# Places for slots, PSUM banks and temporaries by a minimum-cost matching, and a search from kept states, in a hybrid decoder trunk

## The chip, the cores and the metric

The kernel runs on one core of one Trainium2 chip. The metric is device microseconds of one execution. For the kernel before it is the median of three runs. A profile is of one further execution.

A core has five engines that work side by side, each with its own queue of instructions in a fixed order: TensorE (PE, matrix products, with weight loads shown apart as PEld), VectorE (DVE), ScalarE (ACT), GpSimd (POOL) and SyncE (SP, which issues the DMAs here). They wait for each other through semaphores. Matrix products land in PSUM, which has eight banks of 128x512 float32; all else lies in SBUF.

## The reference

Two layers (L = 2) on x of 1024 positions and 1024 channels, all in float32:

```python
for l in range(DEPTH):
    h = rmsnorm(x, attn_norm[l])
    proj = h @ w_in[l]          # 1952 columns, split among four mixers
    y_a = mla_attention(...)    # 4 heads, latent queries and keys, rotary part, causal
    y_b = short_gated_conv(...) # width 3
    y_c = multiscale_pool(...)  # windows 2, 4, 8, 16
    y_d = swa_sink_attention(...)  # window 128, ALiBi, sinks
    mixed = rmsnorm of each of the four groups, times mix_norm[l]
    x = x + mixed @ w_o[l]
    h2 = rmsnorm(x, ffn_norm[l])
    gate, up = jnp.split(h2 @ w_gate_up[l], 2, axis=-1)   # 2 x 2816 columns
    x = x + (jax.nn.silu(gate) * up) @ w_down[l]
return rmsnorm(x, final_norm)
```

## The kernel before

**Data.** Channels lie on the 128 partitions, positions in the free dimension, in two halves (t = 0 and 1) of 512. Every float32 operand of a product is split into a high part, rounded to the format `float32r` of PE, and a low part, the rest. `split` (L299 to L310) makes the high part on ACT (L301, or L306 with a gain) and the low part on DVE (L304, or L307); weights of the attention stage are split in `weights` (ACT L223, DVE L224). One product is then three matmuls, high x high, high x low and low x high: `mm3`, whose matmul is L281. Its sums lie in PSUM under the names `ps_mm`, `ps_s`, `ps_t` and `ps_pv`.

**Stages.** A layer is an attention stage and a feed-forward stage. In the first, PE computes input projections, sliding-window attention (L594 to L655), latent attention (scores L999 to L1001, transposes L1053, values L1065) and the output projection, with many softmax, rotation and split steps on DVE and ACT between them: L380 (products), L1004 and L1007 (maxima), L1018 and L1021 (exponentials), L1037 (scaling). The feed-forward products are made as seven products of 2x2 blocks (B11, B21, B22, N1, N2, T3, T4), whose sums of operands are made ahead: `combine` and `combine_rest` (L1169 to L1186) for the activations, POOL for the weights (L1247, L1249, L1277, L1539). The Silu is at L1459. The end is a last square sum (L364, L368), the last norm (L370 to L376) and the scaling by it (L428).

**Storage.** Three kinds of tiles are given places while the program is written down:

- 47 *slots* of 128x1024 float32 (`u0` to `u46`, shown as `u` in the profile), taken as pairs or halves from the class `Slots` (L57);
- eight PSUM *banks*, by `ps` (L182);
- eight *temporaries* of 128x512, by `tmp` (L191), in three rings: two named `te`, three `tn`, three `tp`. A ring gives its tiles in turn.

A tile that takes a place must wait until the last reader of the tile that had the place is done. So the choice of places decides which waits there are beside those for data.

**The order.** The program is written down once in the order of the code; then a planner makes the order of every engine's queue. The class `Order` (L2103) takes each instruction's duration from formulas (`costs`, L2209, in us), for example these for DVE:

```python
elif op in ("TensorTensor", "TensorReduce"):
    t = 0.15 + n * 0.001045
```

where n is the number of elements of a row. ACT's casts from SBUF are 0.18 + n * 0.00085, a change of ACT's function table is 1.28. `_forward` (L1851) then runs the whole program in a model of five engines. It is used in two ways: with ranks, when each engine takes the ready instruction of the lowest rank, or with fixed orders. `find` (L2255) passes forward and backward to get first ranks; `banks` (L2281) and `spans` (L2296) then give banks and slots from the planned times; the program is written down again with them, and `_search` (L2015) tries changes of the ranks: every second trial lowers the ranks of a chain of instructions that ends at a gap of PE, the other ones shake the ranks in a stretch anywhere in the span. A trial is kept when the mean of the planned ends, over four draws of random delays of the DMAs, is lower. Five rounds of this with 150 trials each are made, and the best of them is searched with 1500 (`TRIALS`, L1808; 40 without the compiler `numba`). The order found is laid upon the queues (`impose`).

A place is chosen greedily before: of the places that are free by the planned start of a tile, the one that came free last; where none is, the one that comes free first (L76 for slots, L291 for banks).

Of the kernel before, what the change touches and what calls it, by code (L numbers as in the profile page):

```python
# [6 lines left out]

# [49 lines left out]
class Slots:  # L57

    def __init__(self, pool, n, spans=None):
        self.pool = pool
        self.spans = spans
        self.made = []
        self.until = [0.0] * n
# [3 lines left out]
        self.dt = [None] * n  # L69

    def place(self):

        if self.spans is None:
            return self.places.popleft()
        start, end = self.spans[len(self.made)]
        i = max(self.places, key=lambda i: u if (u := self.until[i]) <= start else -u)  # L76
        self.places.remove(i)
        self.until[i] = end
        return i

    def pair(self, dt):
        i = self.place()
        self.cur[i] = self.pool.tile([P, 2, HT], dt, name=f"u{i}", tag=f"u{i}", bufs=1)
        self.made.append(self.cur[i].name)
        self.dt[i] = dt
        return 2 * i
# [9 lines left out]
    def free(self, i):  # L96
        h = self.halves[self.dt[i // 2]]
        if i ^ 1 in h:
            h.remove(i ^ 1)
            self.places.append(i // 2)  # L100
        else:
            h.append(i)

    def free_pair(self, i):
        self.places.append(i // 2)
# [25 lines left out]
def trunk_kernel(ctx: ExitStack, tc: tile.TileContext, ins, out, given=None, spans=None, made=None):  # L131
# [10 lines left out]
    slots = Slots(ctx.enter_context(tc.tile_pool(name="slots", bufs=1)), N_U, spans)  # L142
    if made is not None:
        made.append(slots.made)
# [1663 lines left out]
TRIALS = 1500 if numba else 40  # L1808
# [42 lines left out]
def _forward(eng, kind, seen, taken, kb, want, late, hop, start, to, sync, count, rank, fixed, order):  # L1851

    n = eng.size
    left = count.copy()
    ready = np.zeros(n)
    end = np.zeros(n)
    begin = np.zeros(n)
    free = np.zeros(5)
    lk, lv = np.zeros((5, n)), np.zeros((5, n), np.int64)
    nk, nv = np.zeros((5, n)), np.zeros((5, n), np.int64)  # L1860
    ln, nn = np.zeros(5, np.int64), np.zeros(5, np.int64)
    done = np.zeros(5, np.int64)
    flying = np.zeros(LANES)
    issued = 0
    served = 0.0
    lock = 0.0
    table = 0
    for k in range(n):
        if left[k] == 0:
            e = eng[k]  # L1870
            _push(lk[e], lv[e], ln[e], 0.0, k)
            ln[e] += 1
    for _ in range(n):
        best, b = 1e18, -1
        for e in range(5):
            if fixed:
                if done[e] == 0:
                    pass
                i = done[e]
                k = order[e, i] if i < order.shape[1] else -1  # L1880
                if k < 0 or left[k] > 0:
                    continue
                t = max(free[e], ready[k])
            else:
                while ln[e] > 0 and lk[e, 0] <= free[e]:
                    k = lv[e, 0]
                    _drop(lk[e], lv[e], ln[e])
                    ln[e] -= 1
                    _push(nk[e], nv[e], nn[e], rank[k], k)
                    nn[e] += 1  # L1890
                if nn[e] > 0:
                    t = free[e]
                elif ln[e] > 0:
                    t = lk[e, 0]
                else:
                    continue
            if e == SP and issued >= LANES:
                t = max(t, flying[issued % LANES])
            if t < best:
                best, b = t, e  # L1900
        if b < 0:
            return end, begin, False
        t, e = best, b
        if fixed:
            k = order[e, done[e]]
        else:
            while ln[e] > 0 and lk[e, 0] <= t:
                k = lv[e, 0]
                _drop(lk[e], lv[e], ln[e])
                ln[e] -= 1  # L1910
                _push(nk[e], nv[e], nn[e], rank[k], k)
                nn[e] += 1
            k = nv[e, 0]
            _drop(nk[e], nv[e], nn[e])
            nn[e] -= 1
            order[e, done[e]] = k
        done[e] += 1
        more = 0.0
        if kind[k] >= TWO:
            get = max(t + 0.08, lock)  # L1920
            more = get - t - 0.08
            lock = get + max(0.05, seen[k] - (0.16 if kind[k] == TWO else 0.19))
        elif e == ACT and want[k] >= 0:
            if want[k] != table:
                more = 0.0 if kind[k] == TABLE else 1.29
                table = want[k]
        begin[k] = t
        free[e] = t + taken[k] + more
        end[k] = t + seen[k] + more
        if e == SP:  # L1930
            served = max(t + (1.31 if kind[k] == LOAD else 0.41), served) + kb[k] / 322.0
            end[k] = served + 0.82 + late[k]
            flying[issued % LANES] = end[k]
            issued += 1
        for i in range(start[k], start[k + 1]):
# [5 lines left out]
            if left[j] == 0 and not fixed:  # L1941
                _push(lk[eng[j]], lv[eng[j]], ln[eng[j]], ready[j], j)
                ln[eng[j]] += 1
    return end, begin, True
# [51 lines left out]
def _trials(arrays, graph, lates, order, limit):  # L1996

    eng, kind, seen, taken, kb, want, hop = arrays
    start, to, sync, count = graph[:4]
    none = np.zeros(0)  # L2000
    total = 0.0
    for s in range(lates.shape[0]):
        end, _, ok = _forward(
            eng, kind, seen, taken, kb, want, lates[s], hop, start, to, sync, count, none, True, order
        )
        if not ok:
            return 1e18
        total += end.max()
        if total + (lates.shape[0] - 1 - s) * (limit - 2.0) > lates.shape[0] * limit:
            return 1e18  # L2010
    return total / lates.shape[0]
# [3 lines left out]
def _search(arrays, graph, lates, margin, rank, trials, seed):  # L2015
# [5 lines left out]
    width = 0  # L2021
    for e in range(5):
        width = max(width, (eng == e).sum())
    order = -np.ones((5, width), np.int64)
    end, begin, _ = _forward(
        eng, kind, seen, taken, kb, want, margin, hop, start, to, sync, count, rank, False, order
    )
    best = _trials(arrays, graph, lates, order, 1e9)
    first = best
    wins = 0  # L2030
    rank = begin
    trial = -np.ones((5, width), np.int64)
    before = -np.ones(n, np.int64)
    for it in range(trials):
        new = rank.copy()
        if it % 2:
            lo = np.random.random() * end.max()
            hi = lo + math.exp(np.random.random() * 3.5 + 0.7)
            s = math.exp(np.random.random() * 4.0 - 1.5)
            some = np.random.randint(0, 10)  # L2040
            for k in range(n):
                if lo <= begin[k] < hi and (some >= 5 or eng[k] == some):
                    new[k] += s * np.random.randn()
        else:
            last = -1
            gaps = 0.0
            for q in range(width):
                k = order[PE, q]
                if k < 0:
                    break  # L2050
                if last >= 0:
                    gap = begin[k] - begin[last] - taken[last]
                    if gap > 0.04:
                        gaps += gap
                last = k
            pick = np.random.random() * gaps
            last, k = -1, -1
            for q in range(width):
                k = order[PE, q]
                if last >= 0:  # L2060
                    gap = begin[k] - begin[last] - taken[last]
                    if gap > 0.04:
                        pick -= gap
                        if pick <= 0:
                            break
                last = k
            for e in range(5):
                last = -1
                for q in range(width):
                    j = order[e, q]  # L2070
                    if j < 0:
                        break
                    before[j] = last
                    last = j
            s = math.exp(np.random.random() * 4.5 - 1.5)
            for _ in range(np.random.randint(3, 40)):
                new[k] -= s
                p, t = before[k], -1.0
                if p >= 0:
                    t = begin[p] + taken[p]  # L2080
                for i in range(bstart[k], bstart[k + 1]):
                    j = bto[i]
                    r = end[j] + hop[eng[k]] if bsync[i] else begin[j]
                    if r > t:
                        p, t = j, r
# [3 lines left out]
        e1, b1, _ = _forward(  # L2089
            eng, kind, seen, taken, kb, want, margin, hop, start, to, sync, count, new, False, trial  # L2090
        )
        if e1.max() > end.max() + 1.5:
# [390 lines left out]
```

## Time and profile before

| | |
|---|---|
| median of 3 runs | 2044.93 us (2044.12 to 2046.39) |
| the profiled execution's own time | 2045.38 us |
| its span, first to last instruction | 2043.6 us |
| mean granted clock of PE | 0.997 |
| busy: PE, DVE, ACT, POOL | 2022.9, 1578.5, 998.8, 438.9 us |
| instructions (all records) | 26485 |
| DMA traffic | 308.13 MB, mean 151 GB/s |

A line of a group or a wait names the engine, the tile it writes and the line of the code. The line is that of the helper, so L281 stands for nearly all matmuls and L301 and L304 for nearly all splits. "Idle before" is the time for which an engine stood before an instruction, and behind the arrow is what ended it. A row of the timeline begins with the time since the start of the span and the duration. The granted clock is 1 at full speed.

### The profile page before, as it was taken

To read this page: it belongs to the slowest core of one execution; us is meant where nothing else is said; L and a number is where in the kernel's file an instruction comes from. 1 tells how busy PE (TensorE), PEld (TensorE's weight loads), DVE (VectorE), ACT (ScalarE), POOL (GpSimd) and SP (SyncE) were. 2 spreads that over 40 slices of the span, in tenths; PEclk is the share of its full clock that TensorE was granted. 3 is DMA by queue.
4 is the path that set the end of the run, shared out by engine and by line. 5 is a ranking of instruction groups with operands and counts; after the bars stand their busy time and mean duration, and the time that the engine had idled before them with its cause. 6 is when DMAs were issued, how large, how long until landed. Compare 5 with 4: busy or idle time off the path is not lost. (4 is left out here: it accounts for less than half of the span.)

```text
span 2043.6 us, 26485 instructions
## 1 busy us (share of the span) xinstructions
PE 2022.9 (99%) x9398; PEld 1672.6 (82%) x9398; DVE 1578.5 (77%) x2553; ACT 998.8 (49%) x1753; POOL 438.9 (21%) x340
## 2 busy tenths in 40 slices
PE   9999999999999999999999999999999999999998
PEld 7888788878888888888888878888788888888887
DVE  8989979998677777655657999799977777776555
ACT  7458657743333334444434576577433333354342
POOL 0300000025565661000003000000356556500000
PEclk9999999999999999999999999999999999999999
DMA  6310223435555556766513112243455555487542
GB/s 244 127 44 21 84 63 110 149 128 179 179 177 183 176 188 246 259 211 222 176 38 128 56 27 78 65 134 119 145 191 186 177 173 191 169 296 235 195 161 98
DMA packets 144133, 308.13 MB, mean 151 GB/s; under 512 B 14080, under 2 KB 61184, under 8 KB 144000
## 3 DMA queue, kind: packets, MB, share of 16 engines
q1 hardware_dynamic: 144000, 306.43, 44.4%
q8 instruction: 74, 1.21, 0.2%
q14 instruction: 59, 0.48, 0.1%
HBM read 215.67 MB, written 89.65 MB: 149 GB/s over the span
## 5 line engine op out<-in xcount | busy, mean ns | idle before, releaser
L281 PE MATMUL ps_mm<-u,u 128*128 128x512 f32 (+1 forms) x3374 | 843.5, 390 | 7.0 <-ACT u L301 2.8
L281 PEld LDWEIGHTS ps_mm<-u,u 128*128 128x128 f32 x3374 | 615.4, 189 | 129.7 <-ACT u L301 3.6
L281 PE MATMUL ps_s<-u,u 128*128 128x512 f32 x2724 | 652.0, 389 | 0.2 <-DVE u L1214 0.2
L281 PEld LDWEIGHTS ps_s<-u,u 128*128 128x128 f32 x2724 | 510.9, 188 | 108.1 <-DVE u L1214 0.6
L301 ACT CAST u<-u 128x1024 fp32r<-128x1024 f32 (+2 forms) x426 | 361.8, 868 | 478.0 <-PE ps_s L281 116.3
L304 DVE TENSOR_TENSOR u<-u,u 128x1024 fp32r<-128x1024 f32 (+2 forms) x426 | 461.3, 1100 | 154.7 <-ACT u L301 107.0
L281 PE MATMUL ps_t<-u,u 128*128 128x512 f32 (+1 forms) x1092 | 251.9, 377 | 0.0
L281 PEld LDWEIGHTS ps_t<-u,u 128*128 128x128 f32 x1092 | 196.1, 188 | 39.1 <-DVE te L380 0.5
L281 PE MATMUL ps_pv<-u,u 128*128 128x512 f32 x696 | 167.4, 389 | 0.0
L281 PEld LDWEIGHTS ps_pv<-u,u 128*128 128x128 f32 x696 | 130.6, 188 | 27.3 <-DVE tp L1670 0.3
L1277 POOL TENSOR_TENSOR u<-u 128x512 f32<-128x512 f32 x38 | 73.3, 1928 | 226.9 <-DVE u L304 174.2
L1459 ACT ACTIVATE tp<-tp 128x512 f32<-128x512 f32 x76 | 48.0, 632 | 129.3 <-DVE tp L380 129.3
L1062 POOL MEMSET u<- 128x128 f32 x32 | 6.0, 214 | 471.9 <-PE ps_mm L281 250.9
L1247 POOL TENSOR_TENSOR u<-u,u 128x512 f32<-128x512 f32 x38 | 55.6, 1464 | 205.5 <-PE ps_s L281 109.2
L770 POOL TENSOR_TENSOR u<-u,u 128x512 f32<-128x512 f32 x6 | 8.0, 1337 | 413.1 <-ACT sm L628 326.4
L301 ACT CAST u<-ps_t 128x512 fp32r<-128x512 f32 (+3 forms) x132 | 64.8, 502 | 41.3 <-PE ps_t L643 16.6
L1539 POOL TENSOR_TENSOR u<-u 128x352 f32<-128x352 f32 x64 | 79.5, 1244 | 22.4 <-DMA u<-in_w_dn 18.7
L304 DVE TENSOR_TENSOR u<-ps_t,u 128x512 fp32r<-128x512 f32 (+3 forms) x132 | 75.2, 580 | 11.4 <-ACT u L301 10.7
L306 ACT ACTIVATE u<-u,par 128x512 fp32r<-128x512 f32 x92 | 64.6, 719 | 30.7 <-DVE u L380 10.3
L1461 DVE TENSOR_TENSOR tp<-tp,u 128x512 f32<-128x512 f32 x76 | 66.4, 873 | 16.3 <-ACT tp L1459 16.2
L345 ACT ACTIVATE tn<-u 128x512 f32<-128x512 f32 (+1 forms) x91 | 52.6, 597 | 52.2 <-DVE u L1723 45.4
L1249 POOL TENSOR_TENSOR u<-u,u 128x512 f32<-128x512 f32 x38 | 71.8, 1890 | 1.6
(199 smaller groups left out, 2383.5 us busy)
## 6 DMA issues: line engine op xcount, KB each, us to landing
u<-in_w_gu SPq DMA_DIRECT2D x94, 512.0 KB, 4.0
ad<-u SPq DMA_DIRECT2D x154, 256.0 KB, 2.1
u<-ad SPq DMA_DIRECT2D x70, 512.0 KB, 6.0
u<-in_w_dn SPq DMA_DIRECT2D x64, 352.0 KB, 3.3
qd<-u SPq DMA_DIRECT2D x64, 352.0 KB, 2.8
u<-qd SPq DMA_DIRECT2D x32, 512.0 KB, 5.2
u<-in_w_in SPq DMA_DIRECT2D x28, 512.0 KB, 3.9
u<-in_w_dn SPq DMA_DIRECT2D x24, 512.0 KB, 6.5
```

The lines of the kernel that those rows point to most:

```text
L281: pe.matmul(o, w, r, start=start and k == 0 and i == 0, stop=stop and k == n - 1 and i == 2, skip_group_check=again,)
L301: a = act.copy(hi, f)
L304: dve.tensor_tensor(out=lo, in0=f, in1=rd(hi), op=ALU.subtract)
L306: a = act.activation(hi, f, AF.Copy, scale=gain)
L345: act.activation(q, f, AF.Square)
L770: pool.tensor_tensor(out=F.ap(q + 1), in0=a21, in1=a22, op=ALU.add)
L1247: pool.tensor_tensor(out=F.ap(q + 1), in0=a21, in1=a22, op=ALU.add)
L1249: pool.tensor_tensor(out=a21, in0=F.ap(q + 1), in1=a11, op=ALU.add)
L1277: pool.tensor_tensor(out=q4, in0=q4, in1=F.ap(self.raw[1] + 1), op=ALU.add)
L1459: last_silu = act.activation(g, g, AF.Silu)
L1461: dve.tensor_tensor(out=g, in0=g, in1=r, op=ALU.mult)
L1539: pool.tensor_tensor(out=o, in0=a, in1=b, op=ALU.add)
```

## The change

It is in the planner and in the giving of places; the computation, its tiles and its instructions are as they were.

1. `chains` gives places to a list of tiles by a minimum-cost matching: tile k may be followed in its place by tile j. The cost is 1/(gap + 0.5) for a planned gap between the end of k and the start of j, and 10 + 10 x the overlap where j would start before k is over; it is forbidden where the code itself makes j before k is freed. The number of chains is the number of places. It is used for slots (47), banks (8) and temporaries (8).
2. The eight temporaries are one set of places `t0` to `t7`, in place of the three rings.
3. `_forward` becomes `_run`, which can stop at a time and go on from a copied state. The search keeps 60 states along the best order (`STOPS`). A trial starts from the last state ahead of its first change, runs 60 us past the gap at which it is aimed (`HORIZON`), and is dropped there unless PE has done 0.02 us more work than in the best order. All trials are aimed at a gap of PE of over 0.04 us, chosen with a weight by its length.
4. 40000 trials in place of 1500 (4000 in place of 150 in each of the five rounds).
5. The random delays of the trial draws, which were those of the DMAs alone, also hold delays of ACT, DVE and POOL: exponential with a mean of 0.03 us, less that mean.

The core of the diff:

```diff
-    def __init__(self, pool, n, spans=None):
+    def __init__(self, pool, n, homes=None):
...
-        start, end = self.spans[len(self.made)]
-        i = max(self.places, key=lambda i: u if (u := self.until[i]) <= start else -u)
+        i = self.homes[len(self.made)]
         self.places.remove(i)
-        self.until[i] = end
         return i
...
+    temp_of = iter(temps or ())
+
     def tmp(tag="te"):
-        return tpool.tile([P, HT], F32, name=tag, tag=tag, bufs={"te": 2, "tn": 3, "tp": 3}[tag])
+        if temps is None:
+            t = tpool.tile([P, HT], F32, name=tag, tag=tag, bufs={"te": 2, "tn": 3, "tp": 3}[tag])
+        else:
+            t = tpool.tile([P, HT], F32, name=tag, tag=f"t{next(temp_of)}", bufs=1)
+        slots.temps.append(t.name)
+        return t
...
-TRIALS = 1500 if numba else 40
+TRIALS = 40000 if numba else 40
+STOPS, HORIZON = 60, 60.0
...
+        others = np.array([e in ("Activation", "DVE", "Pool") for e in self.engine])
+        self.lates = np.stack(
+            [
+                draw.exponential(moves * 0.5 + others * 0.03, self.n) - others * 0.03
+                for _ in range(4)
+            ]
+        )
...
+        k = at[min(m - 1, np.searchsorted(gaps[:m], np.random.random() * total))]
...
+        _copy(marks[max(0, min(STOPS - 1, int((lo - 1.0) / step)))], work)
...
+        stop = hi + HORIZON
+        _run(arrays, graph, margin, new, False, stop, work)
+        if _worked(arrays, work, stop) < _worked(arrays, s, stop) + 0.02:
             continue
+        _run(arrays, graph, margin, new, False, 1e18, work)
+        if work[2].max() > s[2].max() + 1.5:
+            continue
+        got = _trials(arrays, graph, lates, work[8], best)
...
+    @staticmethod
+    def chains(start, over, born, gone, places):
+
+        n = len(start)
+        gap = start[None, :] - over[:, None]
+        cost = np.where(gap > 0, 1.0 / (np.maximum(gap, 0) + 0.5), 10.0 - 10.0 * np.minimum(gap, 0))
+        cost[gone[:, None] >= born[None, :]] = 1e7
+        full = np.zeros((n + places, n + places))
+        full[:n, :n] = cost
+        after = [int(k) for k in linear_sum_assignment(full)[1]]
+        home, i = [None] * n, 0
+        for k in sorted(set(range(n)).difference(after[:n])):
+            while k < n:
+                home[k] = i
+                k = after[k]
+            i += 1
+        return home
...
     def banks(self, begin, end):
-        free, given = [0.0] * 8, []
...
-        for m in tiles:
-            start = min(begin[k] for k in self.users[m])
-            b = max(range(8), key=lambda b: free[b] if free[b] <= start else -free[b])
...
+        return self.short(tiles, begin, end, 8)
+
+    def temps(self, slots, begin, end):
+        return self.short(slots.temps, begin, end, 8)
...
+    def homes(self, slots, begin, end):
+        _, start, over = self.when(slots.made, begin, end)
+        gone = np.array([slots.gone.get(i, 1 << 30) for i in range(len(slots.made))])
+        return self.chains(start, over, np.array(slots.born), gone, N_U)
...
-        given = plan.banks(begin, end), plan.spans(made, begin, end)
+        given = plan.banks(begin, end), plan.homes(made, begin, end), plan.temps(made, begin, end)
```

More of the change, by code (lines that the diff above doesn't have):

```diff
@@ L2020, in _search @@
     np.random.seed(seed)
[L2021 to L2032, printed above, removed]
+    s = _forward(arrays, graph, margin, rank, width)
+    best = _trials(arrays, graph, lates, s[8], 1e9)
@@ L2033, in _search @@
+    first, rank, wins, stale = best, s[3].copy(), 0, True
+    marks = [_blank(eng, count, width) for _ in range(STOPS)]
+    work = _blank(eng, count, width)
     before = -np.ones(n, np.int64)
+    gaps, at = np.zeros(width), np.zeros(width, np.int64)
     for it in range(trials):
[L2035 to L2048, printed above, removed]
+        if stale:
+            stale = False
+            for e in range(5):
+                for q in range(width):
+                    j = s[8][e, q]
+                    if j < 0:
+                        break
+                    before[j] = s[8][e, q - 1] if q else -1
+            m, total = 0, 0.0
+            for q in range(1, width):
+                k, p = s[8][PE, q], s[8][PE, q - 1]
@@ L2049, in _search @@
                 if k < 0:
                     break
[L2051 to L2075, printed above, removed]
+                gap = s[3][k] - s[3][p] - taken[p]
+                if gap > 0.04:
+                    total += gap
+                    gaps[m], at[m] = total, k
+                    m += 1
```

296 lines of the change are left out of this document (179 added, 117 removed).

## The prediction

> **What bounds the kernel now.** I read the page's busy times first, then a table of five stages, then the list of what TensorE waited for, then the timeline around the longest waits.
>
> ```profile
> span 2043.6 us, 26485 instructions
> PE 2022.9 (99%) x9398; PEld 1672.6 (82%) x9398; DVE 1578.5 (77%) x2553; ACT 998.8 (49%) x1753; POOL 438.9 (21%) x340
> ```
>
> TensorE (PE) bounds the whole. A reordering removes no matmul, so all that it can gain is time in which PE stands still or runs at a lower clock. The stages (attention of layer 1, its feed-forward part, the same for layer 2, the end) say where that time lies. The columns are: length, then busy time and count of PE, weight loads, DVE, ACT and POOL, then granted clock, DMA share and GB/s.
>
> ```profile
> 0.00:459.80 459.80, 452.05 (x2166) 371.09 (x2167) 413.37 (x848) 291.21 (x601) 30.69 (x39) 0.99 0.32 108
> 459.80:1021.80 562.00, 562.00 (x2480) 464.90 (x2479) 390.39 (x443) 225.09 (x301) 189.56 (x133) 1.00 0.59 200
> 1021.80:1481.60 459.80, 456.01 (x2196) 374.33 (x2195) 398.67 (x813) 271.22 (x563) 39.12 (x39) 1.00 0.26 88
> 1481.60:1992.50 510.90, 510.90 (x2255) 422.75 (x2254) 348.28 (x395) 199.09 (x264) 179.57 (x129) 1.00 0.59 197
> 1992.50:2043.60 51.10, 41.91 (x309) 39.57 (x307) 27.82 (x57) 12.21 (x26) 0.00 (x0) 0.95 0.28 97
> ```
>
> The two feed-forward stages are full: 562.0 of 562.0 us and 510.9 of 510.9 us. Over half of the kernel has nothing to give, whatever the order. The first of them also gives PE's pace: 562.0 us / 2480 = 0.227 us a matmul of 512 columns. The profile counts one such matmul as longer than that:
>
> ```profile
> L281 PE MATMUL ps_mm<-u,u 128*128 128x512 f32 (+1 forms) x3374 | 843.5, 390 | 7.0 <-ACT u L301 2.8 <-DVE u L224 2.5 <-ACT u L306 1.0
> ```
>
> A record lasts 0.390 us and the next may start after 0.227, so an idle time in the profile is short by 0.16 us, and a stop below that is not seen at all. The list of PE's waits (us in total, times, longest) is the account of what can be won:
>
> ```profile
> PE ps_mm L281 <- ACT u L301: 2.8, 2, 1.7
> PE ps_mm L281 <- DVE u L224: 2.5, 2, 1.9
> PE ps_pv L497 <- DVE ones L155: 1.1, 1, 1.1
> PE ps_mm L281 <- ACT u L306: 1.0, 1, 1.0
> PE ps_t L1053 <- DVE u L1037: 0.8, 1, 0.8
> PE ps_s L999 <- ACT u L1018: 0.7, 1, 0.7
> PE ps_s L368 <- ACT tn L367: 0.6, 1, 0.6
> PE ps_s L999 <- ACT u L1021: 0.6, 1, 0.6
> PE ps_mm L281 <- DVE u L307: 0.4, 1, 0.4
> PE ps_pv L655 <- ACT u L301: 0.3, 1, 0.3
> PE ps_pv L655 <- DVE u L304: 0.3, 1, 0.3
> PE ps_s L594 <- DVE te L480: 0.2, 1, 0.2
> PE ps_s L281 <- DVE u L1214: 0.2, 1, 0.2
> PE ps_t L361 <- ACT u L301: 0.2, 1, 0.2
> ```
>
> They are 11.7 us in 16 stops. Three of them no order can touch, since nothing else is there to run: the first memset (L497, 1.1), the first normalised inputs (L306, 1.0) and the last square sum (L368, 0.6), 2.7 us together. That leaves 9.0 us in 13 stops. The two longest, from the timeline and from windows laid on the stop and on what follows it:
>
> ```profile
> 208.21 1.22 DVE L224 TENSOR_TENSOR u<-u,u 128x1024 fp32r<-128x1024 f32 x1
> ...
> 209.49 0.79 PE L281 MATMUL ps_mm<-u,u 128*128 128x512 f32 x1 [1.87 <-DVE u L224]
> ```
> ```profile
> 207.60:209.49 1.89, 0.02 (x2) 0.01 (x1) 1.89 (x5) 0.58 (x1) 0.00 (x0) 0.95 0.00 0
> 209.30:212.71 3.41, 3.22 (x8) 2.55 (x9) 3.41 (x10) 2.44 (x7) 0.00 (x0) 0.50 0.39 117
> 424.34:427.75 3.41, 3.41 (x9) 2.63 (x10) 3.41 (x7) 1.68 (x3) 0.00 (x0) 0.50 0.40 137
> ```
>
> At 207.6 us DVE works without a break (1.89 of 1.89 us) and makes the low halves of a weight tile (L224) behind other work; PE waits for them. Right behind the stop the granted clock is 0.50 for 3.41 us. The second stop:
>
> ```profile
> 416.12 5.15 PE L281 MATMUL ps_s<-u,u 128*128 128x512 f32 x22
> ...
> 420.04 1.28 ACT L1459 ACT_TABLE_LOAD   x1
> ...
> 421.87 1.03 ACT L301 CAST u<-u 128x1024 fp32r<-128x1024 f32 x1
> ...
> 422.95 0.74 PE L281 MATMUL ps_mm<-u,u 128*128 128x512 f32 x2 [1.68 <-ACT u L301]
> ```
>
> ACT loads the table for the Silu (L1459) ahead of the cast of the weights for which PE stands. Then again 3.41 us at 0.50. Both stops are an order of ACT or DVE that put the urgent piece behind others.
>
> **The change part by part.** It adds no instruction and removes none: each engine's counts stay. It has four parts.
>
> *The reuse of places* (47 slots, 8 banks). Before, a tile took the place that came free last before the planned start, so its writer stands closest behind the former reader. Now a matching spreads the reuse: a pair costs 1/(gap+0.5), and an overlap costs 10 and more. No page line shows these waits apart from the waits for data. I bound it by the rows of PE's list: at best it takes part in all 9.0 us, at worst one more stop of the longest kind. By itself I take 0; it gives the search its freedom, and the gain is counted there.
>
> *One set of eight temporaries* in place of rings of 2, 3 and 3. The nearest row says that a writer of a temporary had no idle time before it at the entry of the feed-forward part:
>
> ```profile
> L1184 DVE TENSOR_TENSOR tp<-u,u 128x512 f32<-128x512 f32 x6 | 4.1, 685 | 0.0
> ```
>
> So the ring did not hold up this writer. A temporary that is now shared can make a DVE writer wait for an ACT reader of another kind, with DVE's queue behind it, and PE behind that: at most a stop such as L224's, 1.9 us; at best the 0.4 us of a short one. I take 0, the value of the row.
>
> *The search*: 40000 trials in place of 1500, each aimed at a gap of PE (before, every second one fell anywhere in the span, over half of which is full), restarted from a kept state and dropped after 60 us if PE has not done more. Whether that helps on the chip hangs on whether the planner's durations are the chip's. The formulas of `costs` give 0.15 + 512 x 0.001045 = 0.685 us for a DVE addition, and the row above has 685 ns; 0.15 + 1024 x 0.001045 = 1.22 for L224, and the timeline has 1.22; 0.18 + 1024 x 0.00085 = 1.05 for the cast, and it has 1.03; 1.28 for the table load, and it has 1.28. So the planner saw stops of about this size, and they are what a longer search is paid to remove.
>
> *Noise of 0.03 us on ACT, DVE and POOL* in the trial draws: it turns the choice from orders that just fit to orders with a margin. It costs nothing on the chip.
>
> The sum. The two longest stops cost 1.9 + 0.16 + 3.41 x (1 - 0.50) = 3.8 us and 1.7 + 0.16 + 1.7 = 3.6 us, together 7.4. The other eleven hold 9.0 - 3.6 = 5.4, and 11 x 0.16 = 1.8 more: 7.2 us. I take the two long ones as gone, since trials go to gaps by their length, and half of the rest, 3.6 us. Against that stand new stops: the order is new everywhere in both attention stages, and DMA landings and small differences will open gaps that this run doesn't have. I take 3.1 us for them, a little under the half that stays. 7.4 + 3.6 - 3.1 = 7.9 us. The profiled execution took 2045.38 us, its span being 2043.6, and the median of three runs is 2044.93; the gain is a difference, so it is taken from the median: 2044.93 - 7.9 = 2037.0 us.
>
> The half clock is 3.4 of those 7.9 us, and here the Trainium skill speaks against: "TensorE: Matmul & The Clock Gate", in its section on why this matters for your kernels, warns of idle gaps of PE of over about 3 us between bursts as what brings the clock down. By that rule stops of 1.9 and 1.7 us would be harmless and the sum would be 4.5 us. The trace differs: both spells of 0.50 ahead of the last stage lie directly behind the two longest stops, the stage rows leave room for no other (0.99 in the first, 1.00 in the next three), and the stop of 1.1 us (2.8 - 1.7) left none.
>
> **The rivals.**
>
> *DVE is the bound* (chance 0.20). In the stretches around these stops it has no room:
>
> ```profile
> 153.30:204.40 51.10, 51.10 (x236) 41.44 (x235) 50.40 (x95) 42.14 (x80) 0.00 (x0) 1.00 0.08 21
> 255.50:306.50 51.00, 51.00 (x265) 42.48 (x263) 36.67 (x91) 26.66 (x66) 0.70 (x4) 1.00 0.21 63
> 408.70:459.80 51.10, 49.36 (x210) 39.98 (x209) 50.01 (x69) 25.14 (x39) 10.86 (x7) 0.97 0.38 128
> ```
>
> If DVE's work ahead of 209 and 423 us can't shrink, both stops stay. Then 3.6 - 3.1 = 0.5 us remain: 2044.4. Against it: PE could run matmuls with little DVE work there, and at 255 us DVE has 14 us of room in 51.
>
> *Layer 2 falls into the same hole* (0.12), the case on the slow side. Its stops at the same two places are 0.6 (2.5 - 1.9) and 1.1 us, and the clock held. Somewhere between 1.1 and 1.7 us of stop the clock drops. If the new order lets these two grow to layer 1's size and leaves layer 1 as it is, it costs (1.9 - 0.6) + (1.7 - 1.1) + 2 x 1.7 = 5.3 us: 2050.2. For it: the order is new there too, and DVE as full.
>
> *The search closes all 13 stops* and opens none (0.10): 7.4 + 7.2 = 14.6 us, 2030.3.
>
> *The spells of half clock come whatever the stops* (0.05): 7.9 - 3.4 = 4.5 us, 2040.4. The rule of the Trainium skill named above would have it so; the place of the spells speaks against.
>
> *The change doesn't do what it says* (0.03): without the compiler for the search the trials are 40 on both sides; time as before.
>
> **How the numbers follow.** My forecast has the remaining 0.50. About 0.2% (4.1 us) is what a measurement of this kernel can tell from no change. Faster by more: 0.50 + 0.10 + 0.05, less 0.02 for the forecast's own edge, 0.63; within it: 0.20 + 0.03 + 0.02 = 0.25; slower: 0.12. The range goes from 2029.5, the closing of all with a microsecond for stops too short for the list, to 2045.0, which takes in a bound DVE; it leaves out the slow case and a little below, under 0.2.
>
> **What would show it.** Right: counts per engine as now; feed-forward stages still full; PE's list without an entry of 1.5 us or more; no spell of 0.50 ahead of the last 10 us; the list at 5 to 8 us. DVE as the bound: stops behind L224 or L301 of the same length, with DVE at 50 of 51 us. The slow case: a stop above 1.5 us in the second attention stage with 0.50 behind it. The forecast is wrong if PE's list shrinks and the span doesn't, which would mean time lost in stops under 0.16 us that the list can't show.

## The result and the profile after

| | before | after |
|---|---|---|
| median | 2045.12 us (2044.12 to 2046.39, 4 runs) | 2028.23 us (2027.83 to 2028.65, 4 runs) |
| ratio | | 0.9917, 95% interval 0.9900 to 0.9934 |
| profiled span | 2043.6 us | 2026.6 us |
| mean granted clock | 0.997 | 0.999 |

The kernel became 16.9 us faster. (The kernel before has a fourth run here, so its median is 2045.12 us and not the 2044.93 of three.) The forecast was 7.9 us faster, to 2037.0, and its range ended at 2029.5.

The code of the kernel after has 11 lines more ahead of the helpers, so L281, L301, L304 and L224 of before are L292, L312, L315 and L235 here. The head of the page after:

```profile
span 2026.6 us, 26502 instructions
## 1 busy us (share of the span) xinstructions
PE 2012.7 (99%) x9398; PEld 1672.5 (83%) x9398; DVE 1581.3 (78%) x2553; ACT 995.6 (49%) x1753; POOL 449.1 (22%) x340
```

The counts of every engine are as before; the 17 further instructions of the total are of kinds that no engine is busy with. The span is 17.0 us shorter. PE's busy time fell by 2022.9 - 2012.7 = 10.2 us, its idle time by 20.7 - 13.9 = 6.8. What PE waited for, after (us in total, times, longest):

```profile
PE ps_t L372 <- ACT u L312: 1.4, 2, 1.2
PE ps_pv L508 <- DVE ones L159: 1.1, 1, 1.1
PE ps_s L292 <- ACT u L312: 0.9, 1, 0.9
PE ps_s L605 <- ACT tp L628: 0.6, 1, 0.6
PE ps_s L379 <- ACT tn L378: 0.5, 1, 0.5
PE ps_t L292 <- ACT u L312: 0.3, 1, 0.3
PE ps_pv L666 <- DVE u L315: 0.3, 1, 0.3
```

The list holds 5.1 us in 8 stops where it held 11.7 in 16. The three at the start and the end that no order can touch are there (1.1, 0.9, 0.5). None is as long as the two of 1.9 and 1.7 us before, and there is no spell of half clock ahead of the end. By stages, in the windows that the prediction used:

```profile
0.00:459.80 459.80, 456.65 (x2209) 377.21 (x2210) 418.17 (x856) 291.75 (x605) 40.67 (x43) 1.00 0.33 111
459.80:1021.80 562.00, 562.00 (x2481) 465.29 (x2480) 397.32 (x450) 232.44 (x311) 186.19 (x130) 1.00 0.59 200
1021.80:1481.60 459.80, 458.25 (x2226) 381.45 (x2225) 396.82 (x816) 264.63 (x556) 48.18 (x44) 1.00 0.28 92
```

PE begins 2209 matmuls in the first 459.8 us where it began 2166. That is 43 more at 0.227 us, 9.8 us won in layer 1. In the window of layer 2 there are 2226 for 2196, another 6.8 us. The two make 16.6 of the 17.0 us. The feed-forward stage between them is full, as it was.

So 10.2 us of the gain come out of time that counts as busy. The two spells of half clock were 3.4 us of it. Eight stops fewer, each with 0.16 us that a matmul's record covers, are 1.3. The other 5.5 us are what is left by subtraction, and they are put down to stops too short for the list; a lower sum of busy time for the same matmuls is how they are read. The starts of the matmuls in the traces agree. Take the usual distance from one start to the next by width (227, 176, 120 and 109 ns for 512, 384, 256 and 128 columns), leave out the half clock and the end, and add up what exceeds it by 12 to 310 ns each, which is too little for an entry in the list: 28.1 us before, 22.5 after, 5.6 less.

### The profile page after: what moved, and what is told of

It is laid out like the page before. It is cut to its first block, busy times and chain, and to the rows that moved or that the text cites. A ratio compares the mean times of both kernels' runs of the same rounds, so it can differ in the third digit from the quotient of the medians.

```text
span 2026.6 us, 26502 instructions
## 1 busy us (share of the span) xinstructions
PE 2012.7 (99%) x9398; PEld 1672.5 (83%) x9398; DVE 1581.3 (78%) x2553; ACT 995.6 (49%) x1753; POOL 449.1 (22%) x340
## 4 chain that ended last, share of the span: by engine, by line
PE 84%; DVE 3%; ACT 1%; issue 0%; DVEq 0%; ACTq 0%
PE ps_s L292 30%; PE ps_mm L292 29%; PE ps_t L292 11%; PE ps_pv L292 8%; PE ps_pv L1076 2%; PE ps_t L1064 2%; PE ps_s L1010 1%; PE ps_s L1012 1%; PE ps_s L1011 1%; DVE u L391 1%; DVE u L315 0%; ACT u L312 0%; DVE u L318 0%; DVE u L235 0%; PE ps_s L605 0%
## 5 line engine op out<-in xcount | busy, mean ns | idle before, releaser
L292 PE MATMUL ps_mm<-u,u 128*128 128x512 f32 (+1 forms) x3374 | 827.9, 389 | 0.0
L292 PEld LDWEIGHTS ps_mm<-u,u 128*128 128x128 f32 x3374 | 614.3, 188 | 120.6 <-DVE u L318 1.2
L292 PE MATMUL ps_s<-u,u 128*128 128x512 f32 x2724 | 645.6, 389 | 0.9 <-ACT u L312 0.9
L292 PEld LDWEIGHTS ps_s<-u,u 128*128 128x128 f32 x2724 | 511.0, 188 | 108.5 <-ACT u L312 1.6
L315 DVE TENSOR_TENSOR u<-u,u 128x1024 fp32r<-128x1024 f32 (+2 forms) x426 | 460.8, 1099 | 160.5 <-ACT u L312 87.8
L312 ACT CAST u<-u 128x1024 fp32r<-128x1024 f32 (+2 forms) x426 | 362.2, 868 | 420.0 <-PE ps_s L292 94.8
L292 PE MATMUL ps_t<-u,u 128*128 128x512 f32 (+1 forms) x1092 | 247.6, 377 | 0.0
L292 PEld LDWEIGHTS ps_t<-u,u 128*128 128x128 f32 x1092 | 196.6, 188 | 37.6
L292 PE MATMUL ps_pv<-u,u 128*128 128x512 f32 x696 | 165.1, 389 | 0.0
L292 PEld LDWEIGHTS ps_pv<-u,u 128*128 128x128 f32 x696 | 130.6, 188 | 27.1
L1258 POOL TENSOR_TENSOR u<-u,u 128x512 f32<-128x512 f32 x38 | 60.4, 1590 | 228.0 <-DMA u<-in_w_gu 90.9
L1288 POOL TENSOR_TENSOR u<-u 128x512 f32<-128x512 f32 x38 | 61.8, 1626 | 204.0 <-DVE u L315 198.8
L781 POOL TENSOR_TENSOR u<-u,u 128x512 f32<-128x512 f32 x6 | 9.7, 1610 | 374.9 <-PE ps_pv L666 287.5
L1550 POOL TENSOR_TENSOR u<-u 128x352 f32<-128x352 f32 x64 | 84.3, 1318 | 15.7 <-DMA u<-in_w_dn 11.7
L312 ACT CAST u<-ps_t 128x512 fp32r<-128x512 f32 (+3 forms) x132 | 63.4, 505 | 41.7 <-PE ps_t L654 24.4
L391 DVE TENSOR_TENSOR tp<-tp,u 128x512 f32<-128x512 f32 x76 | 81.5, 1072 | 1.6
L315 DVE TENSOR_TENSOR u<-ps_t,u 128x512 fp32r<-128x512 f32 (+3 forms) x132 | 73.9, 577 | 7.6 <-ACT u L312 7.2
L317 ACT ACTIVATE u<-u,par 128x512 fp32r<-128x512 f32 x92 | 64.6, 717 | 25.5 <-DVE u L391 12.9
L1550 POOL TENSOR_TENSOR u<-u,u 128x352 f32<-128x352 f32 x64 | 72.1, 1127 | 4.2
```

The costliest lines, as they stand in the source:

```text
L292: pe.matmul(o, w, r, start=start and k == 0 and i == 0, stop=stop and k == n - 1 and i == 2, skip_group_check=again,)
L312: a = act.copy(hi, f)
L315: dve.tensor_tensor(out=lo, in0=f, in1=rd(hi), op=ALU.subtract)
L317: a = act.activation(hi, f, AF.Copy, scale=gain)
L391: dve.tensor_tensor(out=o, in0=a, in1=b, op=ALU.mult)
L1258: pool.tensor_tensor(out=F.ap(q + 1), in0=a21, in1=a22, op=ALU.add)
```

## The experiments

The prediction put the gain down to the search ("the gain is counted there"). The rival theory is that the places alone did it. The unit of comparison is the kernel before, run beside each experiment on the same chip.

**Places alone** (slots, banks and temporaries matched, old search and noise):

```diff
-        i = max(self.places, key=lambda i: u if (u := self.until[i]) <= start else -u)
+        i = self.homes[len(self.made)]
...
 TRIALS = 1500 if numba else 40
```

The rest of `chains`, for slots, banks and temporaries, goes with it; `_forward` and `_search` stay as before.

> The kernel before, with the matching for slots, banks and the one set of eight temporaries, and with the search, its 1500 trials and its DMA-only noise as they were. If the places made the gain: within 3 us of the kernel after (2028.2), PE's list of waits at 4 to 7 us, no spell of half clock ahead of the end. If the search made it, as the prediction had it: 2041 to 2046, with a stop of over 1.5 us left. A gain shared by both: about 2036.

Measured: 2027.58 us against 2045.79, ratio 0.9908 (0.9892 to 0.9924). That is the whole gain, with the old search of 1500 trials. The list of PE's waits holds 3.8 us, a little under the 4 to 7 expected, and the clock is at full speed up to the end.

**The search alone:**

```diff
-TRIALS = 1500 if numba else 40
+TRIALS = 40000 if numba else 40
+STOPS, HORIZON = 60, 60.0
```

The new `_run`, `_search` and noise go with it; slots, banks and rings stay as before.

> The new search (kept states, 40000 trials aimed at PE's gaps, noise on the engines) with greedy slots and banks and the three rings as before. If the places made the gain: 2040 to 2046, and stops of over 1 us remain. If the search made it: 2028 to 2032, and PE's list at 4 to 7 us.

Measured: 2042.87 us, ratio 0.9981 (0.9972 to 0.9991), 2.9 us faster by the medians. Its page and the top of PE's list:

```profile
span 2042.0 us, 26501 instructions
## 1 busy us (share of the span) xinstructions
PE 2023.2 (99%) x9398; PEld 1670.1 (82%) x9398; DVE 1585.0 (78%) x2553; ACT 999.7 (49%) x1753; POOL 444.6 (22%) x340
```
```profile
PE ps_mm L281 <- ACT u L301: 1.7, 2, 1.1
PE ps_mm L281 <- DVE te L380: 1.2, 1, 1.2
PE ps_pv L497 <- DVE ones L155: 1.1, 1, 1.1
```

This is the most telling run. The search did what the prediction asked of it: the longest stop is 1.2 us, and both spells of half clock are gone (mean clock 0.999). By the prediction's prices that is worth 7.4 us. But PE is busy for 2023.2 us, 0.3 more than before although 3.4 us of half clock are saved. The time went from long stops into stops too short for the list: the sum of 12 to 310 ns excesses, 28.1 us before, is 31.6 us here. With the old places this search spread the waiting and did not remove it. This is also the sign that the prediction named for its being wrong: PE's list shrinks (from 11.7 to 9.0 us) and the span hardly does (2043.6 to 2042.0).

Even the 2.9 us may be no more than the spells. The kernel before, run 43 times beside the experiments, took 2042.25 to 2051.08 us at mean clocks of 0.999 down to 0.995, the longer times mostly at the lower clocks. Its three executions at 0.999 took 2042.25, 2042.28 and 2045.53 us: two of them are as short as the 2042.87 of the search alone. The gain of the places is beyond that: the slowest execution of the kernel after (2028.65) is 13.6 us below the fastest of the kernel before.

**Slots alone, banks alone** (each: the kernel before with the matching for that kind only):

```diff
-        i = max(self.places, key=lambda i: u if (u := self.until[i]) <= start else -u)
+        i = self.homes[len(self.made)]
...
```
```diff
-            b = max(range(8), key=lambda b: free[b] if free[b] <= start else -free[b])
...
+        return self.short(tiles, begin, end, 8)
```

> The kernel before with the matching for the 47 slots alone; greedy banks, three rings, old search. If slots carry the gain of the places: 2028 to 2033. If banks do: 2042 to 2046. If each carries a share: 2035 to 2040.

> The kernel before with the matching for the eight PSUM banks alone; greedy slots, three rings, old search. If banks carry the gain of the places: 2028 to 2033. If slots do: 2042 to 2046. If each carries a share: 2035 to 2040, and with the slots' share it makes about the 17 us.

Measured: slots 2039.96 us, ratio 0.9970 (0.9958 to 0.9982); banks 2036.26, ratio 0.9952 (0.9935 to 0.9969). Each carries a share, 5.8 and 9.5 us, together 15.3 of the 18.2 that the places brought with the one set of temporaries. The same two edits turned round, one at a time, in the kernel after:

> The kernel after with one part undone: slots go greedily, in the order of the code, to the place that came free last before the planned start; banks and temporaries stay matched. Slots alone had brought 5.8 us. If the shares add up: 2033 to 2036. If banks alone are what is needed: 2027 to 2031. If either part fails without the other: above 2037.

> The kernel after with one part undone: greedy banks; slots and temporaries stay matched. Banks alone had brought 9.5 us. If the shares add up: 2036 to 2039. If slots are what is needed: 2027 to 2031. If either part fails without the other: above 2040.

Measured: 2032.80 us, ratio 0.9927 (0.9911 to 0.9944), without the matching of the slots; 2034.31, ratio 0.9935 (0.9921 to 0.9950), without that of the banks. By the medians that is 4.6 and 6.1 us above the kernel after; by the ratios, which compare within a chip, 2.0 and 3.7. So undoing either loses less than it brought alone, and both times lie between the expected ranges: the shares don't add up. Each may in part repair what the other would; but the kernel after also has the new search and the joined temporaries, which the single runs lack, and no run here separates that. How much of each is not settled to better than these 2 to 3 us.

**The temporaries left in rings**, slots and banks matched, old search:

```diff
-        given = plan.banks(begin, end), plan.homes(made, begin, end), plan.temps(made, begin, end)
+        given = plan.banks(begin, end), plan.homes(made, begin, end), None
```

> As the kernel with the places alone, but the temporaries stay in their rings of 2, 3 and 3: slots and banks matched, old search. If the joined set of temporaries is worth nothing by itself, as the prediction took it: 2027 to 2029, like the places together (2027.6). If it adds to them: 2029.5 to 2033.

Measured: 2029.27 us, ratio 0.9924 (0.9909 to 0.9938). It lies between the two expectations, above the places with one set by 1.7 us in the medians and by 0.0016, or 3.3 us, in the ratios, whose intervals overlap. The joined set is worth something between nothing and about 3 us; this run can't say more.

**What in the matching counts.** It does two things that the greedy choice does not: it avoids overlaps over the whole list at once, and among places without overlap it takes the one that has been free longer. Two edits are to tell them apart:

```diff
-        cost = np.where(gap > 0, 1.0 / (np.maximum(gap, 0) + 0.5), 10.0 - 10.0 * np.minimum(gap, 0))
+        cost = np.where(gap > 0, 0.001 * np.maximum(gap, 0), 10.0 - 10.0 * np.minimum(gap, 0))
...
-        i = max(self.places, key=lambda i: u if (u := self.until[i]) <= start else -u)
+        i = min(self.places, key=lambda i: self.until[i])
```

The first is in the matching with the old search; the second is in the kernel before, for slots, and in the same way for banks.

> Slots, banks and temporaries matched with the same price of an overlap, but with the price of a gap turned round: 0.001 a us, so that among places without overlap the one freed last is taken, as the greedy choice did. If the gain is that overlaps are avoided: 2027 to 2031. If it is that reuse is spread, so that writers stand far behind old readers: 2038 to 2046.

> The kernel before with one edit: slots and banks go greedily to the place that came free first, so that reuse is spread as far as a greedy choice can, with no care for overlaps. If spreading is what counts: 2028 to 2036. If avoiding overlaps over the whole list is what counts: 2042 or slower, since old places are used up and later tiles have to take busy ones.

Measured: the tight matching 2034.46 us, ratio 0.9948 (0.9933 to 0.9963); the oldest free place 2052.84, ratio 1.0031 (1.0014 to 1.0047). Neither single theory of the first was right: avoiding overlaps over the whole list, with the one set of temporaries that goes with it, brings 9.9 us by the medians, and the spread that the tight matching lacks is another 6.9, down to the 2027.6 of the places alone, which were run on another chip. But spreading by a greedy choice, one tile at a time, makes the kernel slower, as its expectation had it. That choice too takes a free place while there is one; what it lacks is the view of the tiles still to come. The list of PE's waits of that run begins like this, with stops at the values and transposes of the sliding window in place of the two long ones:

```profile
PE ps_pv L655 <- ACT u L301: 2.2, 3, 1.3
PE ps_pv L655 <- DVE u L304: 2.1, 4, 0.8
PE ps_t L643 <- DVE tp L632: 2.0, 4, 0.8
```

**A wait for a place, seen directly.** The low halves of the attention weights (L224, later L235) are made by DVE from a DMA's landing and from ACT's high half. Nothing of theirs comes from PE. Where the profile says that DVE sat idle before them until PE was done, it waited for PE's last reading of the tile that had the place. The groups of this line, before and after (count, then busy and mean ns, then idle before it and what ended it):

```profile
L224 DVE TENSOR_TENSOR u<-u,u 128x1024 fp32r<-128x1024 f32 (+1 forms) x43 | 48.1, 1121 | 14.5 <-PE ps_mm L281 9.1 <-PE ps_t L281 3.8 <-ACT u L223 1.5
```
```profile
L235 DVE TENSOR_TENSOR u<-u,u 128x1024 fp32r<-128x1024 f32 (+1 forms) x43 | 48.8, 1138 | 6.6 <-PE ps_mm L292 3.1 <-ACT u L234 3.0 <-DMA u<-in_w_in 0.3
```

Before, DVE stood for 9.1 + 3.8 = 12.9 us in front of these 43 splits for the sake of a place; after, for 3.1. That is one side only. The high halves of the same tiles are made by ACT from the DMA's landing alone (L223, later L234), and their lines, before and after, go the other way:

```profile
L223 ACT CAST u<-u 128x1024 fp32r<-128x1024 f32 (+1 forms) x43 | 41.5, 968 | 16.1 <-DMA u<-in_w_in 5.6 <-DVE u L734 3.7 <-DVE u L224 3.3
```
```profile
L234 ACT CAST u<-u 128x1024 fp32r<-128x1024 f32 (+1 forms) x43 | 41.1, 968 | 26.3 <-PE ps_mm L292 17.6 <-PE ps_t L1064 2.8 <-DMA u<-in_w_in 2.6
```

By the same reading ACT waits for a place for 20.4 us after; before, no more than 16.1 - 12.6 = 3.5 us of its idle time can be such. So the waits for places in front of these weights did not become fewer. Much of them moved from DVE, which is busy for 413 of the first 460 us, to ACT, which is busy for 291. That a wait costs less there is likely, but no run here shows it. DVE's line by itself, in the view of its instructions and of what ended their idle time, of the search alone, of the tight matching and of the places alone:

```profile
  PE ps_mm L281: 12.1, 3
  PE ps_t L281: 1.3, 1
  ACT u L223: 0.8, 3
```
```profile
  ACT u L234: 7.0, 4
  PE ps_mm L292: 3.9, 2
  PE ps_pv L666: 0.9, 1
```
```profile
  ACT u L234: 6.2, 5
  PE ps_t L292: 1.4, 1
  POOL u L783: 0.6, 1
  PE ps_mm L292: 0.2, 1
```

Waits for PE are 13.4 us with the new search on old places (2042.9 us), 4.8 with the tight matching (2034.5) and 1.6 with the places (2027.6). In the kernel after with the slots as before it is 8.1. But the line doesn't follow the time everywhere: it is 0.4 us with slots alone (2040.0), 2.3 with banks alone and greedy slots (2036.3), and 5.9 in the slowest kernel of all, the oldest free place (2052.8). So it shows that waits for places exist and how they look, and it is not a measure of the gain. Waits for a bank, the kind with the largest share by itself, are not seen directly in any view here. The long stop of before at 207.6 us began with DVE behind in its work, in front of this very line; that such waits had put DVE behind there is argued from these sums, not shown for that one stop.

**Is it luck?** A search with random trials gives another order for another seed. The edits are to seeds and counts only, the last one in the kernel with the places alone:

```diff
-        found = plan.search(trials // 10, r)
+        found = plan.search(trials // 10, 100 + r)
...
-TRIALS = 40000 if numba else 40
+TRIALS = 1500 if numba else 40
...
-TRIALS = 1500 if numba else 40
+TRIALS = 4000 if numba else 40
```

> The kernel before with other seeds for its searches; the greedy places are found anew in each round. If the old places hold the kernel at its level whatever the search draws: 2041 to 2049. If the kernel before was an unlucky draw: below 2038, and the shares of the parts would have to be taken from that.

> The kernel after with other seeds for its searches. It tells how much of a difference is the luck of one search: 2026 to 2031 if the gain is one of the places; a spread of over 5 us would put the shares of slots, banks and temporaries in doubt.

> The kernel after with 1500 trials in place of 40000 (150 in each round). If the places alone made the gain: 2026 to 2031, like the kernel after (2028.2). If the many trials are needed on top of them: 2032 or slower.

> The matched places (slots, banks, one set of temporaries) with the search of the kernel before, its DMA-only noise, and 4000 trials in place of 1500. With 1500 it took 2027.6. If the search is at its end: 2026 to 2028.5. If more trials of the old kind still help: 2022 to 2026.

Measured: the kernel before with other seeds 2047.21 us, ratio 1.0002 (0.9991 to 1.0013); the kernel after with other seeds 2027.02, 0.9906 (0.9891 to 0.9921); the kernel after with 1500 trials 2027.51, 0.9910 (0.9893 to 0.9926); the places with 4000 trials of the old search 2028.03, 0.9911 (0.9896 to 0.9926). Five orders on matched places lie between 2027.0 and 2028.2 us, whatever the search. None of them can be told from the kernel after. With other seeds the kernel before kept its time, a stop of 1.9 us behind L224 and two spells of half clock ahead of the end. The matched places were not run without any search, so what the old search still does on them is open.

**The half clock.** Two spells of it were 3.4 us of the prediction's sum, with the rule of the Trainium skill that the prediction names against them. A kernel with nothing of the trunk in it makes 100 stops of PE of known lengths:

```python
for i in range(REPEATS):
    for links, width in LEVELS:
        n += 1
        pe.matmul(q, w, late, start=True, stop=True)
        act.activation(t[:, :width], q[:, :width], AF.Copy, scale=0.5)
        for _ in range(links - 1):
            act.activation(t[:, :width], t[:, :width], AF.Copy, scale=0.5)
        act.activation(late[:, :64], t[:, :64], AF.Copy, scale=0.5)
        pe.matmul(q, w, late, start=True, stop=True)
        for _ in range(44 + (n * 7) % 15):
            pe.matmul(p, w, r, start=True, stop=True)
```

> No part of the trunk: 100 stops of PE of ten lengths, from about 0.5 to 3.5 us, each made by a chain of ScalarE operations that a matmul waits for, between bursts of 44 to 58 matmuls; the output is not the reference's. If a stop of 1.7 us and more brings a spell of half clock, as read from the trace before: spells behind most stops above 1.7 us, none below 1.1. If only idle times of over 3 us do: spells behind the longest level alone. If it depends on where the stop falls: spells behind a share of the stops that grows with the length.

It measured nothing of this: in its trace part of each burst runs ahead of the matmul that waits, and PE's longest stop behind ScalarE was 0.3 us. With the bursts reading what the chain writes (`r` replaced by `late`):

> No part of the trunk: 100 stops of PE of ten lengths from about 0.5 to 3.5 us, each made by a chain of ScalarE operations; now every matmul of the bursts between them (44 to 58 matmuls) reads what the chain writes, so that none can run during a stop; the output is not the reference's. If a stop of 1.7 us and more brings a spell of half clock: spells behind most stops above 1.7 us, none below 1.1. If only idle times of over 3 us do: spells behind the longest level alone. If it depends on where the stop falls: spells behind a share of the stops that grows with the length.

Now there are stops from 0.6 to 3.5 us. PE's waits, then windows laid on two stops of the same length and on what follows each:

```profile
PE probe L45 <- ACT late L44: 195.3, 100, 3.5
```
```profile
105.54:107.58 2.04, 0.01 (x1) 0.00 (x0) 0.00 (x0) 1.79 (x4) 0.00 (x0) 1.00 0.00 0
108.92:112.33 3.41, 3.41 (x10) 2.65 (x9) 0.00 (x0) 0.00 (x0) 0.00 (x0) 0.50 0.00 0
404.60:406.64 2.04, 0.00 (x1) 0.01 (x1) 0.00 (x0) 1.79 (x4) 0.00 (x0) 1.00 0.00 0
406.64:413.47 6.83, 6.83 (x30) 5.66 (x31) 0.00 (x0) 0.00 (x0) 0.00 (x0) 1.00 0.01 2
```

Two stops of 2.04 us: behind the first, the clock is 0.50 for 3.41 us, behind the second it stays full. Over the whole trace, none of the 50 stops of up to 1.7 us has a spell behind it; of those of 2.0, 2.3, 2.7, 3.0 and 3.5 us, ten each, 4, 6, 6, 8 and 10 have one (counted where a spell begins between the start of the stop and 3.6 us behind its end). So it is the third of the expected outcomes, from about 2 us on, and not only over 3.

## Why the prediction was wrong

The direction was right, and each sign that the text named for "right" is there: counts unchanged, feed-forward stages full, no stop of 1.5 us, no spell of half clock, PE's list at 5.1 us within "5 to 8". The cause was wrong, and with it the size.

*The reuse of places: "By itself I take 0; it gives the search its freedom, and the gain is counted there."* This is the step that failed: it put the places at nothing of their own and gave the gain to the search. Places alone brought 18.2 us (0.9908), the search alone 2.9 (0.9981). The bound beside it ("at best it takes part in all 9.0 us") was too small as well. The text said that no line shows waits for places apart from waits for data; for a writer without an input from the engine it waits for, one does, and L224 sits idle for 12.9 us until PE is done, though none of its data comes from PE. Such a row would have shown that the waits are there, though not what they cost. Through which waits the places make their 18.2 us stays open.

*The two longest stops gone, 7.4 us.* Right for the kernel after. But the run with the search alone has them gone too, and keeps 2.9 us of it. A stop is worth its price only if the work behind it moves up; here the time came back in pieces, most of them too short for the list.

*"Half of the rest, 3.6 us", and 3.1 us of new stops.* Of the 7.2 us in the eleven smaller stops and the new ones 6.7 were to remain. There are 5 stops apart from the three fixed ones, 5.1 - 2.5 = 2.6 us, with 0.16 us each 3.4. This term was 3.3 us too careful. With the 5.5 us of the next point it is nearly all of the 9.0 us between the forecast gain and the measured one.

*Stops too short for the list.* They entered the low end with one microsecond (2030.3 - 1 is 2029.3, where the text has 2029.5); they gave 5.5. That is why even the case in which all 13 stops close (2030.3) lay above the measured time.

*The temporaries: 0.* Not refuted: something between nothing and about 3 us.

*The planner's durations* agreed with the trace, as said; the conclusion that a longer search is what removes the stops did not follow from it. On matched places 1500 trials do as well as 40000 (2027.5 and 2028.2).

*The rivals.* DVE as the bound is refuted: in the first 459.8 us it is busy for 418.2 us, 4.8 more than before, and PE does 43 matmuls more. DVE had more room than its busy share ahead of the stops made it look. Layer 2 did not fall into the hole: its longest stop is 1.2 us. The closing of all stops was nearest to the time, but by a way that it did not name: 8 stops stayed, and time outside the list went. That the spells come whatever the stops is refuted twice: they went with the stops, and the 50 short stops of the test brought none. The Trainium skill's warning in "TensorE: Matmul & The Clock Gate", under why this matters for your kernels, of gaps over about 3 us, doesn't hold here as a limit: 4 of 10 stops of 2.0 us had a spell behind them. The prediction's own limit, a stop somewhere between 1.1 and 1.7 us, doesn't hold either: ten stops of 1.7 us had none.

## What to carry to other kernels

When storage is shared out by a program, the choice of places makes waits of its own, and here a longer search over orders did not take them away: repair the places first, by a choice over the whole list that avoids overlap and then spreads reuse. Such waits are found by looking for a writer that is idle until an engine is done from which it takes no data; look at all writers of the tiles, since a wait that leaves one engine may stand on another. And a list of stops is not the whole account of a pipelined engine: compare its sum of busy time for the same instructions, since short stops hide there.

## What the runs showed of the hardware that was not expected

The half clock follows PE's idle time in a stretch of 3.41 us on a fixed grid, and not the longest single stop. In the kernel after with slots as before, the longest stop of PE is 1.3 us, and yet a spell follows it; a second stop came right behind:

```profile
1095.40 0.30 PE L654 MATMUL ps_t<-cst,tp 128*128 128x128 f32 x1 [1.29 <-DVE tp L643]
1095.46 0.47 PE L292 MATMUL ps_mm<-u,u 128*128 128x512 f32 x1
1096.66 0.69 PE L654 MATMUL ps_t<-cst,tp 128*128 128x128 f32 x2 [0.73 <-DVE tp L643]
```
```profile
1093.12:1096.53 3.41, 1.53 (x8) 0.77 (x6) 3.26 (x5) 1.47 (x3) 3.26 (x3) 1.00 0.00 0
1096.54:1099.95 3.41, 3.29 (x10) 2.81 (x11) 2.73 (x5) 0.95 (x2) 3.41 (x2) 0.50 0.35 96
```

In the 3.41 us ahead of the spell PE was busy for 1.53, idle for 1.88. Single stops of up to 1.7 us in the test brought no spell, and those of 2.0 us brought one in 4 of 10.

The traces show why the same length does and does not bring one. In every trace the spells begin a whole number of times 3.413 us behind the first row of the clock's record, to within 4 ns; in the test all 35 do. So the stretches lie on a grid that runs freely. These are the grid's stretches around the two stops of 2.04 us:

```profile
105.51:108.92 3.41, 1.37 (x7) 1.12 (x7) 0.00 (x0) 1.79 (x4) 0.00 (x0) 1.00 0.00 0
402.46:405.88 3.42, 2.14 (x10) 1.44 (x8) 0.00 (x0) 1.12 (x3) 0.00 (x0) 1.00 0.00 0
405.88:409.29 3.41, 2.65 (x12) 2.18 (x13) 0.00 (x0) 0.67 (x2) 0.00 (x0) 1.00 0.00 0
```

The first stop lies within one stretch and leaves PE 1.37 us of work in it; the second is cut in two, and each stretch keeps over 2 us. Over the whole test, each of the 34 stretches at full clock with PE busy for 1.38 us or less has a spell behind it, and none with 1.56 us or more has. In the trunk's profiles the border is less sharp: the stretches ahead of the eight spells had PE busy for 1.2 to 2.05 us, and the least busy ones without a spell for 1.9 and 2.0. The Trainium skill describes such a window, free-running and of about 3.4 us, in "TensorE: Matmul & The Clock Gate", Part 1. The traces agree: here every spell ahead of the end lasts 3.41 us or twice that. Where the grid lies against the program differs from run to run (its first row is 4.5 us behind the start of the span before, 4.2 after). That fits the kernel before taking 2042 to 2051 us at clocks of 0.999 down to 0.995: whether its long stops cost a spell is in part luck.
